# Reciprocal roots by ScalarE's square root and one Newton step, and softmax maxima negated by the reduction and scaled by ScalarE

## The chip, the cores and the metric

The kernel runs on one core of a Trainium2 chip. The metric is the device time of one execution in microseconds; where several executions of a kernel are timed, their median counts. The engines of the core are named as in the profile: PE is TensorE's matmul and PEld its weight load, DVE is VectorE, ACT is ScalarE, POOL is GpSimd and SP is SyncE, which issues most of the transfers.

## What is computed

Two blocks of two layers each over 512 tokens of width 1024. The first block has a second stream of 256 context tokens. What matters here are its root mean square norms, its softmaxes and the places where they stand:

```python
def rmsnorm(x, gain=None):
    xf = x.astype(jnp.float32)
    y = xf * lax.rsqrt(jnp.mean(xf * xf, axis=-1, keepdims=True) + EPS)
    ...

def attend(q, k, v):
    s = jnp.einsum('bkgqd,bksd->bkgqs', q, k).astype(jnp.float32) * (HEAD_DIM ** -0.5)
    p = jax.nn.softmax(s, axis=-1).astype(v.dtype)
    return jnp.einsum('bkgqs,bksd->bkgqd', p, v)

def first_block(...):
    for l in range(DEPTH):
        ...
        hx = rmsnorm(x) * (1 + sc_a) + sh_a
        hc = rmsnorm(ctx) * (1 + mc[1]) + mc[0]
        ...                       # mixer: Fourier, attention (normed heads), gated recurrence
        x = x + g_a * (jnp.concatenate([fx, ax, rx], axis=-1) @ w_out[l])
        x = x + g_f * swiglu(rmsnorm(x) * (1 + sc_f) + sh_f, w_gate[l], w_up[l], w_down[l])
        ...
    return rmsnorm(x, final_norm)

def second_block(...):
    for l in range(DEPTH):
        hdn = swiglu_2(rms_norm(x, norm_pre[l, 0]), ...)
        x = x + 0.5 * rms_norm(hdn, norm_post[l, 0])
        ...                       # l = 0: block attention (MoBA) and a linear recurrence; l = 1: a convolution
        x = x + rms_norm(mix, norm_post[l, 1])
        hdn = swiglu_2(rms_norm(x, norm_pre[l, 2]), ...)
        x = x + 0.5 * rms_norm(hdn, norm_post[l, 2])
    return x
```

## The kernel before

Activations are kept feature by feature: 8 tiles of 128 features, with the tokens along the free axis. Every fp32 product is made of three matmuls on rounded halves (lines 245 to 247): a value is split into a rounded high part, by an ACT copy, and the rest, by a DVE subtraction (`split`, lines 212 and 213; weights at lines 230 and 232, once they have landed).

The program is a row of phases: the first mixer (Mix1, layer 0), its feed-forward block ffn0, the second mixer (layer 1), ffn1, and then four feed-forward blocks (ffn2) with two other mixers between them: MixE with MoBA and a linear recurrence, MixO with a convolution. Inside a mixer several streams (dense projections, two halves of the recurrence `hgrn`, Fourier, attention) are woven together by declared costs. Between two phases `boundary` runs: the last products of a phase for one chunk of 256 tokens are followed by the norm and the splits of the next phase for that chunk, while TensorE goes on with the other chunk.

A norm runs so: ACT squares the tiles (line 297), POOL or DVE adds them (line 299), PE sums over features by a product with a column (line 311), `rsqrt_small` makes the reciprocal root of a few columns, DVE spreads it (line 284), PE transposes it (line 286), and then it multiplies tiles. `rsqrt_small` begins with the addition of EPS (line 269, or 271 with a column). Lines 272 and 273 make a first guess from the bits of the number, and a loop of three Newton steps follows (lines 275 to 277): 12 DVE operations on 2 to 12 columns. It is called 51 times: once in the opening, 16 times in the two mixers (heads of keys and queries, `hgrn`), and otherwise in norms at the phase boundaries.

`softmax_tile` handles 128 queries against all their keys: the maximum of a row (line 562, DVE), the negative scaled maximum (line 565 where the scale is the constant 0.125, line 567 where it is a column), and on ACT the exponential, which takes both and also adds up the row (line 568). There are 80 such tiles with a column (attention of the two mixers) and 32 with the constant (MoBA). The exponentials are transposed by PE (line 1011).

A buffer comes from one of two hand-run stores, `arena` and `rarena`, with a third part, `room`, that is lent to either. The order in which the instructions of an engine stand is set when the program is built, by a scheduler that runs a timeline of its own over the dependencies; so a change at one place can move instructions elsewhere. The build puts an ACT table load ahead of an ACTIVATE whose function is not in the set that was loaded last.

Of the kernel before, what the change touches and what calls it, by code (L numbers as in the profile page):

```python
# [10 lines left out]
I32 = mybir.dt.int32  # L11
U8 = mybir.dt.uint8
AF = mybir.ActivationFunctionType
ALU = mybir.AluOpType
AX = mybir.AxisListType
# [48 lines left out]
class _Arena:  # L64
# [32 lines left out]
    def fr(self, *bufs):  # L97
        for b in bufs:
            if isinstance(b, (list, tuple)):
                self.fr(*b)  # L100
                continue
            h = b.home
            assert (h.freed[b.o:b.o + b.u] == np.inf).all()
            h.clock += 1
            h.freed[b.o:b.o + b.u] = h.clock
# [38 lines left out]
def _body(tc, xc, cvec, w_ada, w_in, w_four, w_out, gu, dn, cols, ab_in, ab_out, gates, c_in, c_out,  # L144
          k_id, k_hs, k_lm, k_cm, k_dft, k_dftc, k_bd, k_rope, xsc, out, stop=None, dbg=None, mark=lambda n: None):
    nc = tc.nc
    V, A, G, PE, SP = nc.vector, nc.scalar, nc.gpsimd, nc.tensor, nc.sync
# [9 lines left out]
    with es:  # L157
# [34 lines left out]
        def hlrows(n, count):  # L192
            r = [(alr(n, True), alr(n, True)) for _ in range(count)]
            return r, r
# [12 lines left out]
        def pick(tag):  # L207

            return G if tag in ONPOOL else V

        def split(h, lo, src, eng=V):
            A.activation(h, src, AF.Copy)  # L212
            eng.tensor_tensor(lo, src, h.bitcast(F32), ALU.subtract)  # L213
# [50 lines left out]
        def rsqrt_small(ps, n, eps=None):  # L264

            b = al(192)
            v, y, t = (b.f[:, i * 64:i * 64 + n] for i in range(3))
            if eps is None:
                V.tensor_scalar(v, ps, EPS, None, op0=ALU.add)
            else:  # L270
                V.tensor_tensor(v, ps, eps, ALU.add)
            V.tensor_scalar(t.bitcast(I32), v.bitcast(I32), 1, None, op0=ALU.logical_shift_right)
            V.tensor_scalar(y.bitcast(I32), t.bitcast(I32), -1.0, float(0x5F3759DF), op0=ALU.mult, op1=ALU.add)
            for _ in range(3):
                V.tensor_tensor(t, v, y, ALU.mult)
                V.scalar_tensor_tensor(t, t, -0.5, y, op0=ALU.mult, op1=ALU.mult)
                V.scalar_tensor_tensor(y, t, 1.5, y, op0=ALU.add, op1=ALU.mult)
            return b, y

        def bcast_r(r, ps, tb, c, heads):  # L280
# [88 lines left out]
        class Ffn(Phase):  # L369
# [11 lines left out]
            def begin(self, ch):  # L381
                if self.act is None:
                    mark(self.name)
                    self.actb, self.act = hlrows(self.w, KD)
                if self.beginf:
                    self.beginf(ch)

# [155 lines left out]
        def rope(xs, tabs, shift, tag):  # L543
            n = S
            sh, m1 = al(n), al(n)
            V.stream_shuffle(sh.f, xs, shift)
            G.tensor_tensor(m1.f, xs, tabs[0].f, ALU.mult)
            pick("r1" + tag).tensor_tensor(sh.f, sh.f, tabs[1].f, ALU.mult)
            pick("r2" + tag).tensor_tensor(xs, m1.f, sh.f, ALU.add)
            fr(sh, m1)  # L550
# [7 lines left out]
        def softmax_tile(sp, nk, sc, pn, sm):  # L558

            b = al(64)  # L560
            mx, nb = (b.f[:, i:i + 1] for i in range(2))
            V.reduce_max(mx, sp[:, :nk], axis=AX.X)
            if sc is None:
                sc = 0.125
                V.tensor_scalar(nb, mx, -sc, None, op0=ALU.mult)
            else:
                V.scalar_tensor_tensor(nb, mx, -1.0, sc, op0=ALU.mult, op1=ALU.mult)
            A.activation(pn, sp[:, :nk], AF.Exp, bias=nb, scale=sc, accum_out=sm)
            fr(b)

# [747 lines left out]
        class MixE(Mix2):  # L1318
# [36 lines left out]
            def dense(self):  # L1355
# [40 lines left out]
                for j in range(4):  # L1396
                    for d, b in ((self.q, j), (self.k, 4 + j)):
                        f = al(S)
                        self.proj(b, f.f)
                        rope(f.f, self.rope, sh8, "E")  # L1400
                        d[j], = hlrows(S, 1)[0]
                        split(d[j][0].r, d[j][1].r, f.f, pick("seE"))
                        fr(f)
                        yield 5.2
                    f = al(S)
                    self.proj(8 + j, f.f)
                    pt = transposed(f.f, S)
                    fr(f)
                    v = self.v[j] = alr(1024, True)
                    vr = v.r.rearrange("p (t g c) -> p t g c", t=4, g=2)  # L1410
                    vf = v.f.rearrange("p (t g c) -> p t g c", t=4, g=2)
                    for t in range(4):
                        src = pt.f[:, t * 128:t * 128 + 128].rearrange("p (g c) -> p g c", g=2)
                        A.activation(vr[:, t, :, 0:64], src, AF.Copy)
                        V.tensor_tensor(vr[:, t, :, 64:128], src, vf[:, t, :, 0:64], ALU.subtract)
                    pf_(pt)
                    self.flags.add(f"qkv{j}")
                    yield 5.2
# [488 lines left out]
```

## Time and profile before

| what | value |
|---|---|
| median of 3 runs | 3865.65 us (3865.28 to 3867.86) |
| the profiled execution: its time, its span | 3867.11 us, 3865.3 us |
| mean granted clock of TensorE | 0.972 |
| instructions | 49381 |
| ACT table loads in the program | 15 |

Everything that is read from a trace comes from the one profiled execution. Times in it count from the start of the span. A row of a timeline gives the start, the duration, the engine, the source line and the operation, what it writes and reads with shapes, how many instructions the row merges, and in brackets how long the engine had been idle before and what ended that. A busy PE is not a PE at its peak, since matmuls overlap.

### The profile page before, as it was taken

How to read it: one execution, taken by the hardware profiler on the slowest of the kernel's cores; microseconds unless marked ns; L12 is line 12 of the kernel's file. 1: busy time of each engine (PE TensorE's matmuls, PEld its weight loads, DVE VectorE, ACT ScalarE, POOL GpSimd, SP SyncE). 2: the span in 40 equal slices, each digit the busy share in tenths (PEclk: the TensorE clock that was granted, in tenths of full speed). 3: DMA queues.
4: the chain of work that ended last, by engine and by line, in shares of the span. 5: the costliest groups of instructions: out<-in, count | busy, mean ns of one | idle time of the engine just before them, and what ended most of it. 6: DMA issues, size and time to landing. Idle time of an engine off the chain costs nothing.

```text
span 3865.3 us, 49381 instructions
## 1 busy us (share of the span) xinstructions
PE 3669.9 (95%) x19960; PEld 3152.5 (82%) x19960; DVE 1955.3 (51%) x3502; ACT 1350.5 (35%) x2265; POOL 571.9 (15%) x507
## 2 busy tenths in 40 slices
PE   6988799999999888999999998999999999999998
PEld 5776688888887767888988896798889888888887
DVE  8687756533245676433442357653336333735233
ACT  4234643432233355322332234443224222323231
POOL 3332112431013310000100031030002001211001
PEclk9898999999999899999999998999999999999999
DMA  5222104443211212332233222123323322323222
GB/s 203 65 89 66 58 30 158 157 139 132 67 43 53 60 54 82 97 98 80 71 112 101 67 86 74 50 88 109 102 73 99 104 95 74 107 70 100 94 94 73
DMA packets 95829, 345.18 MB, mean 89 GB/s; under 512 B 10864, under 2 KB 14064, under 8 KB 95600
## 3 DMA queue, kind: packets, MB, share of 16 engines
q1 hardware_dynamic: 95024, 341.50, 27.4%
q8 instruction: 156, 2.56, 0.3%
q14 instruction: 73, 0.60, 0.0%
q10 hardware_dynamic: 576, 0.52, 0.0%
HBM read 334.64 MB, written 4.19 MB: 88 GB/s over the span
## 4 chain that ended last, share of the span: by engine, by line
PE 57%; DVE 3%; ACT 1%; DMA 1%; POOL 0%; issue 0%; DVEq 0%; POOLq 0%; ACTq 0%; SPq 0%
PE psum L245 17%; PE psum L246 17%; PE psum L247 17%; DVE rarena L1168 1%; PE psum L262 1%; PE psum L261 1%; PE psum L260 1%; PE psum L311 1%; PE psum L1477 1%; DVE arena L1213 1%; DMA arena<-gu 0%; POOL arena L1215 0%; DVE rarena L232 0%; PE psum L1491 0%; PE psum L1011 0%
## 5 line engine op out<-in xcount | busy, mean ns | idle before, releaser
L245 PE MATMUL psum<-rarena,room 128*128 128x512 f32 (+1 forms) x3041 | 1073.2, 354 | 18.0 <-ACT rarena L212 8.5
L246 PE MATMUL psum<-rarena,room 128*128 128x512 f32 (+1 forms) x3041 | 1073.0, 353 | 3.8 <-DVE rarena L213 2.3
L247 PE MATMUL psum<-rarena,room 128*128 128x512 f32 (+1 forms) x2955 | 1052.7, 357 | 0.8 <-DVE room L232 0.8
L247 PE MATMUL psum<-rarena 128*128 128x512 f32 (+1 forms) x2118 | 743.7, 352 | 11.6 <-DVE rarena L232 11.5
L245 PE MATMUL psum<-rarena 128*128 128x512 f32 (+1 forms) x2032 | 727.7, 359 | 17.8 <-ACT rarena L230 7.7
L246 PE MATMUL psum<-rarena 128*128 128x512 f32 (+1 forms) x2032 | 725.2, 357 | 1.3 <-DVE rarena L213 1.3
L245 PEld LDWEIGHTS psum<-rarena,room 128*128 128x128 f32 x3041 | 579.2, 191 | 97.0 <-ACT rarena L212 8.7
L246 PEld LDWEIGHTS psum<-rarena,room 128*128 128x128 f32 x3041 | 579.5, 191 | 80.6 <-DVE rarena L213 2.8
L247 PEld LDWEIGHTS psum<-rarena,room 128*128 128x128 f32 x2955 | 562.5, 190 | 79.9 <-DVE room L232 1.0
L232 DVE TENSOR_TENSOR room<-arena,room 128x1024 fp32r<-128x1024 f32 (+2 forms) x252 | 325.2, 1297 | 519.2 <-PE psum L246 207.6
L230 ACT ACTIVATE room<-arena 128x1024 fp32r<-128x1024 f32 (+2 forms) x290 | 319.5, 1110 | 664.0 <-PE psum L247 169.1
L299 POOL TENSOR_TENSOR arena<-arena 128x256 f32<-128x256 f32 x170 | 144.4, 856 | 2286.3 <-ACT arena L297 2065.0
L247 PEld LDWEIGHTS psum<-rarena 128*128 128x128 f32 x2118 | 407.7, 193 | 63.8 <-DVE rarena L232 12.8
L245 PEld LDWEIGHTS psum<-rarena 128*128 128x128 f32 x2032 | 391.9, 193 | 73.6 <-ACT rarena L230 8.8
L246 PEld LDWEIGHTS psum<-rarena 128*128 128x128 f32 x2032 | 391.7, 193 | 52.6 <-DVE rarena L213 1.5
L230 ACT ACTIVATE rarena<-arena 128x1024 fp32r<-128x1024 f32 (+2 forms) x141 | 157.7, 1123 | 361.6 <-PE psum L247 89.7
L232 DVE TENSOR_TENSOR rarena<-arena,rarena 128x1024 fp32r<-128x1024 f32 (+2 forms) x104 | 137.5, 1322 | 262.6 <-ACT rarena L230 129.3
L212 ACT ACTIVATE rarena<-arena 128x256 fp32r<-128x256 f32 (+2 forms) x254 | 130.3, 530 | 241.4 <-DVE arena L410 202.6
L213 DVE TENSOR_TENSOR rarena<-arena,rarena 128x256 fp32r<-128x256 f32 (+2 forms) x247 | 143.0, 596 | 95.9 <-ACT rarena L212 95.8
L410 DVE TENSOR_TENSOR arena<-arena,psum 128x512 f32<-128x512 f32 (+1 forms) x170 | 100.2, 598 | 176.5 <-PE psum L247 168.2
L297 ACT ACTIVATE arena<-arena 128x256 f32<-128x256 f32 (+1 forms) x274 | 107.0, 412 | 211.2 <-DVE arena L1239 87.6
L500 POOL TENSOR_TENSOR arena<-arena 128x1024 f32<-128x1024 f32 x48 | 120.7, 2521 | 230.8 <-DMA arena<-w_ada 141.1
(360 smaller groups left out, 4234.1 us busy)
## 6 DMA issues: line engine op xcount, KB each, us to landing
arena<-gu SPq DMA_DIRECT2D x264, 512.0 KB, 3.7
arena<-dn SPq DMA_DIRECT2D x80, 704.0 KB, 4.1
arena<-w_ada SPq DMA_DIRECT2D x57, 512.0 KB, 3.8
room<-w_ada SPq DMA_DIRECT2D x39, 512.0 KB, 3.7
room<-w_in SPq DMA_DIRECT2D x31, 512.0 KB, 3.6
arena<-c_in SPq DMA_DIRECT2D x24, 512.0 KB, 3.5
arena<-dn SPq DMA_DIRECT2D x16, 448.0 KB, 3.8
room<-ab_in SPq DMA_DIRECT2D x13, 512.0 KB, 3.6
```

Source lines behind the costliest of these rows:

```text
L212: A.activation(h, src, AF.Copy)
L213: eng.tensor_tensor(lo, src, h.bitcast(F32), ALU.subtract)
L230: A.activation(h.r, r.f, AF.Copy)
L232: (G if wlo[1] < wlo[0] else V).tensor_tensor(lo.r, r.f, h.f, ALU.subtract)
L245: PE.matmul(ps, h[:, s], ah, start=k == 0, stop=False)
L246: PE.matmul(ps, h[:, s], al_, start=False, stop=False)
L247: PE.matmul(ps, lo[:, s], ah, start=False, stop=k == nk - 1)
L260: PE.matmul(o, w[0].r[:, s], ah, start=False, stop=False)
L297: A.activation(sq.f, src, AF.Square)
L299: (V if self.fast else G).tensor_tensor(self.parts[0].f, self.parts[0].f, sq.f, ALU.add)
L410: V.tensor_tensor(s.f, s.f, pu, ALU.mult)
L500: G.tensor_tensor(t.f, r.f, sic[q].f, ALU.mult)
```

## The change

`rsqrt_small` loses the guess from the bits and two of the three Newton steps. In their place ACT takes a square root, DVE a reciprocal, and one Newton step follows: five DVE operations with the addition at its head, and one on ACT. In `softmax_tile` the reduction negates the maximum itself. Where the scale is a column, ACT multiplies by it. Where it was the constant 0.125, nothing is multiplied; instead MoBA's queries are scaled when they are split, which takes the factor along in the ACT copy and makes the DVE subtraction one of three operands. In ffn0, whose head has one hidden tile, the rows for it are allocated at the start of the phase instead of at its first head.

```diff
--- before.py
+++ after.py
@@ -269,12 +269,11 @@
                 V.tensor_scalar(v, ps, EPS, None, op0=ALU.add)
             else:
                 V.tensor_tensor(v, ps, eps, ALU.add)
-            V.tensor_scalar(t.bitcast(I32), v.bitcast(I32), 1, None, op0=ALU.logical_shift_right)
-            V.tensor_scalar(y.bitcast(I32), t.bitcast(I32), -1.0, float(0x5F3759DF), op0=ALU.mult, op1=ALU.add)
-            for _ in range(3):
-                V.tensor_tensor(t, v, y, ALU.mult)
-                V.scalar_tensor_tensor(t, t, -0.5, y, op0=ALU.mult, op1=ALU.mult)
-                V.scalar_tensor_tensor(y, t, 1.5, y, op0=ALU.add, op1=ALU.mult)
+            A.activation(y, v, AF.Sqrt)
+            V.reciprocal(y, y)
+            V.tensor_tensor(t, v, y, ALU.mult)
+            V.scalar_tensor_tensor(t, t, -0.5, y, op0=ALU.mult, op1=ALU.mult)
+            V.scalar_tensor_tensor(y, t, 1.5, y, op0=ALU.add, op1=ALU.mult)
             return b, y
 
         def bcast_r(r, ps, tb, c, heads):
@@ -382,6 +381,8 @@
                 if self.act is None:
                     mark(self.name)
                     self.actb, self.act = hlrows(self.w, KD)
+                    if self.hf == 1:
+                        self.hid = hlrows(self.w, 1)[0]
                 if self.beginf:
                     self.beginf(ch)
 
@@ -558,13 +559,12 @@
         def softmax_tile(sp, nk, sc, pn, sm):
 
             b = al(64)
-            mx, nb = (b.f[:, i:i + 1] for i in range(2))
-            V.reduce_max(mx, sp[:, :nk], axis=AX.X)
+            nb = b.f[:, 0:1]
+            V.reduce_max(nb, sp[:, :nk], axis=AX.X, negate=True)
             if sc is None:
-                sc = 0.125
-                V.tensor_scalar(nb, mx, -sc, None, op0=ALU.mult)
+                sc = 1.0
             else:
-                V.scalar_tensor_tensor(nb, mx, -1.0, sc, op0=ALU.mult, op1=ALU.mult)
+                A.activation(nb, nb, AF.Copy, scale=sc)
             A.activation(pn, sp[:, :nk], AF.Exp, bias=nb, scale=sc, accum_out=sm)
             fr(b)
 
@@ -1399,7 +1399,11 @@
                         self.proj(b, f.f)
                         rope(f.f, self.rope, sh8, "E")
                         d[j], = hlrows(S, 1)[0]
-                        split(d[j][0].r, d[j][1].r, f.f, pick("seE"))
+                        if d is self.q:
+                            A.activation(d[j][0].r, f.f, AF.Copy, scale=0.125)
+                            V.scalar_tensor_tensor(d[j][1].r, f.f, 0.125, d[j][0].f, op0=ALU.mult, op1=ALU.subtract)
+                        else:
+                            split(d[j][0].r, d[j][1].r, f.f, pick("seE"))
                         fr(f)
                         yield 5.2
                     f = al(S)
```

What the scheduler makes of it is shown at three places. First VectorE in the opening, around the first root. `mod` holds the modulation columns, made by products with rows of w_ada. Before:

```order
L269 TENSOR_SCALAR arena<-psum 128x6
L272 TENSOR_SCALAR arena<-arena 128x6
L273 TENSOR_SCALAR arena<-arena 128x6
L275 TENSOR_TENSOR arena<-arena 128x6
L276 SCALAR_TENSOR_TENSOR arena<-arena 128x6
...
L1641 SCALAR_TENSOR_TENSOR room,mod_65<-room,arena 128x1024
...
L1648 TENSOR_SCALAR mod_65<-psum,COL 128x2
...
L284 COPY room<-arena 128x128 x6
```

After:

```order
L269 TENSOR_SCALAR arena<-psum 128x6
L273 RECIPROCAL arena<-arena 128x6
L274 TENSOR_TENSOR arena<-arena 128x6
L275 SCALAR_TENSOR_TENSOR arena<-arena 128x6
L276 SCALAR_TENSOR_TENSOR arena<-arena 128x6
L283 COPY room<-arena 128x128 x6
L1645 SCALAR_TENSOR_TENSOR room,mod_65<-room,arena 128x1024 x2
```

Two products with w_ada and their additions, which stood inside the chain, now stand behind the copies that end it (line 1645 is line 1641 of before).

Second ScalarE in the attention of the first mixer, beside the readout of `hgrn` (lines 943 and 944 copy and square its output). Before:

```order
L568 ACTIVATE room,arena<-psum,room,arena 128x768
L568 ACTIVATE room,arena<-psum,arena 128x768
L943 ACTIVATE room<-psum 128x256
L944 ACTIVATE room<-psum 128x256
L212 ACTIVATE rarena<-psum 128x512 x6
```

After:

```order
L568 ACTIVATE room,arena<-psum,room,arena 128x768
L943 ACTIVATE room<-psum 128x256
L944 ACTIVATE room<-psum 128x256
L567 ACTIVATE arena<-arena 128x1
L272 ACT_TABLE_LOAD
L272 ACTIVATE room<-room 128x4
L568 ACT_TABLE_LOAD
L568 ACTIVATE room,arena<-psum,arena 128x768
L212 ACTIVATE rarena<-psum 128x512 x6
```

A scaled maximum (line 567) stands ahead of its exponential, and between the two are the root of the readout and two table loads.

Third ScalarE at a boundary between two ffn2 blocks (1183 copies a broadcast root out of PSUM, 407 and, after, 408 is the silu). Before:

```order
L230 ACTIVATE room<-arena 128x1024
L1167 ACTIVATE rarena<-arena,COL 128x256
L297 ACTIVATE arena<-arena 128x256 x2
L1183 ACTIVATE arena<-psum 128x256
L407 ACTIVATE arena<-arena 128x256 x3
L212 ACTIVATE rarena<-arena 128x256 x3
L230 ACTIVATE room<-arena 128x1024 x3
```

After:

```order
L1183 ACTIVATE arena<-psum 128x256
L408 ACT_TABLE_LOAD
L408 ACTIVATE arena<-arena 128x256 x3
L212 ACTIVATE rarena<-arena 128x256 x3
L230 ACTIVATE room<-arena 128x1024 x3
L272 ACT_TABLE_LOAD
L272 ACTIVATE arena<-arena 128x2
L230 ACTIVATE rarena<-arena 128x1024
```

The table is changed for the silus and back for the next root; before, no load stood here. In the whole program there are 52 loads where there were 15.

## Rows read from the trace of the kernel before

**Rows 1.** Page, part 1: busy time of each engine, its share, instructions.
```profile
PE 3669.9 (95%) x19960; PEld 3152.5 (82%) x19960; DVE 1955.3 (51%) x3502; ACT 1350.5 (35%) x2265; POOL 571.9 (15%) x507
```
**Rows 2.** Windows: length, busy PE, PEld, DVE, ACT, POOL, clock, DMA.
```profile
0.00:100.00 100.00, 65.44 (x325) 56.49 (x327) 84.30 (x120) 45.70 (x68) 35.10 (x20) 0.97 0.57 197
260.00:500.00 240.00, 196.42 (x1056) 154.99 (x1055) 172.69 (x368) 123.37 (x250) 41.51 (x33) 0.89 0.18 55
1310.00:1530.00 220.00, 194.16 (x1081) 160.74 (x1080) 141.81 (x260) 111.44 (x209) 33.38 (x30) 0.94 0.18 55
2600.00:2850.00 250.00, 250.00 (x1105) 207.07 (x1104) 91.92 (x99) 74.75 (x90) 0.00 (x0) 1.00 0.30 98
```
**Rows 3.** Waits of PE: us in total, times, longest.
```profile
PE psum L1011 <- ACT room L568: 26.8, 24, 3.6
...
PE psum L1000 <- ACT room L568: 13.8, 10, 3.4
...
PE psum L286 <- DVE arena L284: 9.8, 9, 2.7
...
PE psum L286 <- DVE room L284: 6.7, 2, 3.5
```
**Rows 4.** Windows, DVE busy: lines 275, 276, 277, 272, 273, 567 in turn.
```profile
0.00:3865.30 3865.30, 41.79 (x153) 0.97 0.28 89
0.00:3865.30 3865.30, 33.35 (x153) 0.97 0.28 89
0.00:3865.30 3865.30, 35.28 (x153) 0.97 0.28 89
0.00:3865.30 3865.30, 18.98 (x51) 0.97 0.28 89
0.00:3865.30 3865.30, 20.63 (x51) 0.97 0.28 89
0.00:3865.30 3865.30, 17.23 (x80) 0.97 0.28 89
```
**Rows 5.** Timeline of DVE: first and last operation of the last chain.
```profile
3853.42 0.16 DVE L271 TENSOR_TENSOR arena<-psum,arena 128x2 f32<-128x2 f32 x1 [1.59 <-PE psum L311]
...
3855.59 0.16 DVE L277 SCALAR_TENSOR_TENSOR arena<-arena 128x2 f32<-128x2 f32 x1
```
**Rows 6.** Groups by line: operations on few columns (busy us, mean ns).
```profile
L579 DVE RECIPROCAL arena<-arena 128x8 f32<-128x8 f32 (+1 forms) x16 | 3.1, 195 | 12.4 <-ACT room L568 8.5 <-ACT arena L568 3.8
...
L1302 ACT ACTIVATE arena<-COL 128x4 f32<-128x4 f32 x1 | 0.2, 206 | 0.0
```
**Rows 7.** Timeline: from a scaled maximum to its exponential.
```profile
442.75 0.16 DVE L567 SCALAR_TENSOR_TENSOR room<-room,arena 128x1 f32<-128x1 f32 x1
...
443.00 0.99 ACT L568 ACTIVATE room<-psum,room,arena 128x768 f32<-128x768 f32 x1 [2.42 <-DVE room L567]
```
**Rows 8.** Timelines of DVE and POOL: inside the opening's chain.
```profile
18.94 2.19 DVE L273 TENSOR_SCALAR arena<-arena 128x6 int32<-128x6 int32 x1
...
29.35 0.36 DVE L284 COPY room<-arena 128x128 f32<-128x128 f32 x2
...
18.76 2.34 POOL L1643 TENSOR_TENSOR room<-room,arena 128x1024 f32<-128x1024 f32 x1 [18.32 <-DVE arena L269]
```
**Rows 9.** Timeline of ACT: two table loads and what follows.
```profile
1141.84 1.28 ACT L645 ACT_TABLE_LOAD   x1
1143.98 0.38 ACT L645 ACTIVATE arena<-psum 128x256 f32<-128x256 f32 x1 [0.86 <-PE psum L247]
...
2570.31 1.28 ACT L407 ACT_TABLE_LOAD   x1
2571.61 1.03 ACT L407 ACTIVATE arena<-arena 128x256 f32<-128x256 f32 x3
```
**Rows 10.** Timeline of PE: stalls ahead of two phases.
```profile
1151.86 0.80 PE L245 MATMUL psum<-rarena,room 128*128 128x256 f32 x2 [4.19 <-ACT rarena L212]
...
1543.48 1.44 PE L245 MATMUL psum<-rarena,room 128*128 128x256 f32 x5 [4.30 <-ACT rarena L212]
```

## The prediction

> **What bounds the kernel now.** I read the busy shares first: TensorE is busy for 95% of the span, VectorE for 51%, ScalarE for 35% [rows 1]. So the change, which touches no matmul, can only act on the 195 us in which TensorE stands still (3865.3 - 3669.9). The table by stage says where these are [rows 2]: 34.6 us in the first 100, 43.6 in the first mixer's attention (260 to 500), 25.8 in the second mixer's (1310 to 1530), and none in the middle of a feed-forward block (250.00 of 250). Then the waits of TensorE say for whom [rows 3]: for the exponentials of line 568 on ScalarE (26.8 + 13.8 us), and at line 286, the transposes that broadcast a reciprocal root (9.8 + 6.7 us). The change works on both.
>
> **What the roots cost, and what takes their place.** There are 51 calls of rsqrt_small. Lines 272 and 273 run once a call, lines 275 to 277 three times; together they hold VectorE for 41.79 + 33.35 + 35.28 + 18.98 + 20.63 = 150.0 us [rows 4]. An undisturbed chain is the last one: from 3853.42 to 3855.75, 2.33 us for 12 operations, 0.194 each [rows 5]. The new chain has 5 VectorE operations (the addition, the reciprocal, three of the one step), so 0.97 us; the reciprocal is taken at that size since line 579's took 0.195 [rows 6]. A square root on a few columns is priced by line 1302, 0.21 us [rows 6]. A crossing from VectorE to ScalarE takes 0.09 (line 567 ends at 442.91, line 568 starts at 443.00 [rows 7]), and there are two. That makes 1.36 us, 0.97 less than before, if ScalarE is free and has the right table. Disturbed chains lose more: the opening's took 10.4 us from line 273 at 18.94 to the copies of line 284 at 29.35, because single operations stood for some 2 us while GpSimd multiplied (line 273 for 2.19, until 21.13; GpSimd's ran until 21.10 [rows 8]), and fewer operations meet fewer of these. VectorE loses about 150.0 - 51 x 4 x 0.194 = 110 us, and 80 x 0.215 = 17 more at line 567 [rows 4]; the 32 at line 565 are taken at the same size, 7.
>
> **What ScalarE gains.** 51 roots and 80 scaled maxima at 0.21 are 27.5 us. The order shows 52 table loads where there were 15; a load takes 1.283, shown as 1.28 [rows 9], so 37 more are 47.5 us. Altogether 75 us on an engine that is 65% idle. A load stands behind what precedes it on ScalarE, but need not wait for the operand: at 1141.84 one ran 0.86 us ahead of its matmul [rows 9]. Most new loads stand like that in the order, so most are hidden while ScalarE idles. The Trainium skill speaks against this change: "ScalarE: Activation LUTs", section "Table sets: the hidden batching unit", says to group calls by table set, and this change alternates roots with exponentials, sigmoids and silus. The same page, section "What ACT_TABLE_LOAD costs", has 2.66 us a switch, with a drain; by it the 37 loads would be an estimated 98 us. The row at 2571.61 disagrees: the next ACTIVATE began 0.02 us after its load had ended [rows 9].
>
> **The sum, place by place.**
> 1. *Opening.* What is left of the chain after line 273's start shrinks from 10.4 us to about 1.2, or 3.4 with one collision of 2.2. The load is behind the silus of line 1663 and has no wait of its own. What is late next are the products with w_ada on VectorE, which is 84% busy there [rows 2] and loses about 7 us of work too. Bounds 0 and -7 (10.4 - 3.4); I take **-5**, nearer to the gain since VectorE sets the pace there.
> 2. *End.* Behind the last chain TensorE waits 2.7 us, the longest of its waits in [rows 3] at line 286 for the arena, and nothing covers it; both last roots share one load. **-1**.
> 3. *Other waits at line 286.* 9.8 + 6.7 - 3.5 - 2.7 (the two longest, terms 1 and 2) = 10.3 us in nine places; VectorE is full there with the scaled copies around the chain, and 7 of 12 chain operations go. But the root now queues behind ScalarE's squares and splits. Bounds 0 and -10.3; **-5**.
> 4. *Norms ahead of the second mixer and of its feed-forward block.* TensorE waits 4.19 and 4.30 us for splits that a root chain precedes [rows 10]. Five more loads fall near the first of these. Bounds +3 (two loads exposed) and -8.5; **-3**.
> 5. *Softmax in the two mixers.* Before: maximum, 0.16 on VectorE, 0.09, exponential [rows 7]. After: maximum, 0.09, 0.21 on ScalarE, exponential on the same engine. The chain keeps its length within 0.1 us, so its 80 tiles give nothing directly. VectorE, the busier engine here (172.69 against 123.37 us of 240 [rows 2]), gets lighter. Against that the order puts a root with its two loads between exponentials three times (2 x 1.28 + 0.21 = 2.8 us each, 8.3 in all). Bounds: +30 (80 x 0.21 = 16.8, the 8.3, and the mixers' four other new loads, 5.1, all exposed) and -25 (VectorE's relief ends over a third of the 69 us of idle TensorE); I take **-2**, near nought because the rows put TensorE's waits about as much on ScalarE as on VectorE.
> 6. *MoBA.* 32 times one VectorE operation less ahead of the exponential, 0.19 each, 6 us if nothing hid them; TensorE has other streams to run: **-1**. The four query splits only take a factor along, on the same engines: 0.
> 7. *Boundaries between feed-forward blocks.* 26 of the new loads, up to four at one boundary. TensorE has whole products queued there, and a silu load stood at 2570.31 in the kernel before [rows 9] while line 407 is nowhere among the engines that TensorE waited for. **0**; without that cover 26 x 1.28 = +33, of which I leave a few us in the range. The earlier allocation of ffn0's first hidden rows only changes an address: 0.
>
> Together -17 us. The profiled execution took 3867.11 us (span 3865.3 and 1.8 around it), 1.5 above the median of 3865.65; from the median, **3849 us**. Its own spread: 3838 to 3857.9, from half of terms 1, 3 and 4 to all of them.
>
> **The rivals.**
> A. *Hidden.* The roots' waits are filled by the next late thing (a weight split, a w_ada load), only the end and a part of the opening remain: -1 - 5, 3860 us. For it: TensorE's queue is in order, and what stands ahead of line 286 is often late as well. Against it: line 286 is named as a wait of its own eleven times.
> B. *ScalarE becomes the late engine in the mixers (slower).* The copies and loads of term 5 sit in ScalarE's order between exponentials, and TensorE already waits 40.6 us for these [rows 3]. All exposed: +30, less the 14 us of terms 1 to 4: 3882 us. It decides from nearly three quarters exposed: (14 + 7.7) of 30. For it: the waits by name. Against it: ScalarE is 51% busy in these windows.
> C. *VectorE's relief counts fully.* Term 5 at -25: 3826 us. For it: VectorE is at 72% in the first attention and its operations are the ones that GpSimd stalls. Against it: about half the waits end on ScalarE.
> D. *A load also empties ScalarE.* Were each to cost its 1.28 once more, the ten in the mixers would add 12.8 us: -17 + 13, 3862 us. The row at 2571.61 [rows 9] speaks against it. The drain is the skill's rule, "What ACT_TABLE_LOAD costs" again.
> That the change would not do what it says is out: the order has the 51 reciprocals and 80 scaled copies.
>
> **How the numbers follow.** Forecast 0.42, A 0.20, B 0.17, C 0.17, D 0.04. A measurement of this kernel tells about 0.2% (7.7 us) from no change. Faster: forecast and C, 0.59; same: A and D, 0.24; slower: B, 0.17. The range of 3822 to 3876 holds forecast, A and D, two thirds of C and a third of B, and leaves out 0.17.
>
> **What would show it.** Right: TensorE's wait at line 286 down from 16.5 us to under 8; the opening's copies of line 284 some 7 us earlier; VectorE's busy time down by 110 to 140 us, ScalarE's up by 70 to 80; last root chain about 1.4 us. Wrong: TensorE waiting more than 45 us for line 568 (B); silu or sigmoid loads named as releasers at the block boundaries (term 7); those copies no earlier than 27 us (term 1); idle time behind every load (D).

## The result, and the profile after

| | before | after |
|---|---|---|
| median | 3865.73 us | 3817.85 us (3813.81 to 3824.42) |
| ratio to before | | 0.9877, 95% interval 0.9860 to 0.9894 |
| profiled execution: time, span | 3867.11, 3865.3 us | 3813.81, 3811.9 us |
| TensorE busy, and the rest of the span | 3669.9, 195.4 us | 3644.4, 167.5 us |
| mean granted clock | 0.972 | 0.977 |

The change saves 48 us, where 17 were forecast; 3817.85 lies 4 us below the range's lower end of 3822. The lines have moved: 286 is now 285, 284 is 283, 562 is 563, 1701 is 1705, 272 is ScalarE's root, 273 the reciprocal and 567 ScalarE's scaled copy.

Part 1 of the page of the kernel after answers to [rows 1]:

```profile
PE 3644.4 (96%) x19960; PEld 3135.4 (82%) x19960; DVE 1879.7 (49%) x3033; ACT 1426.0 (37%) x2433; POOL 576.0 (15%) x507
```

ScalarE gained 75.5 us (75 were worked out), VectorE lost 75.6 (110 to 140 were). The number of matmuls is the same, yet TensorE is busy for 25.5 us less and stands still for 27.9 less: the 53.4 us of the span come from both by halves. The profiled execution is the fastest of the four. Over all four the granted clock was 0.974 to 0.977 with a mean of 0.976, over all executions of the kernel before 0.969 to 0.975 with a mean of 0.972. The product of busy time and clock, of which more below, was 3567 and 3561 us. An estimate from these for the 48 us between the medians is some 20 for the busy time (3567/0.972 - 3561/0.976) and 28 for the stand-still. That the busy time of untouched matmuls would fall was nowhere in the prediction.

TensorE's waits (engine, line, who was waited for: us in total, times, longest us). Before, beside [rows 3]:

```profile
PE psum L247 <- DVE rarena L232: 11.5, 3, 5.8
...
PE psum L1701 <- ACT rarena L1693: 3.7, 2, 3.0
```

After:

```profile
PE psum L1011 <- ACT room L568: 24.8, 24, 2.7
PE psum L1705 <- ACT rarena L1697: 10.6, 2, 6.8
PE psum L285 <- DVE arena L283: 9.7, 9, 3.0
PE psum L247 <- DVE rarena L232: 6.4, 2, 5.8
...
PE psum L1000 <- ACT room L568: 3.6, 6, 1.5
...
PE psum L285 <- DVE room L283: 1.6, 2, 0.9
```

The wait at the transposes went from 16.5 to 11.3 us, not to under 8. The wait of line 1000, whose products need the place that an exponential frees, went from 13.8 to 3.6. The wait of the opening for the splits of line 1697 (1693 before) grew from 3.7 to 10.6.

Three stages by windows, cut at the same instructions: the dense part of mixer 2, the first attention, and the second, which follows that dense part. Before (window, length, then busy us and count of PE, PEld, DVE, ACT, POOL, the granted clock, DMA share, GB/s):

```profile
1179.80:1335.70 155.90, 145.35 (x774) 121.27 (x775) 83.96 (x178) 44.41 (x85) 55.39 (x63) 0.89 0.17 53
277.10:498.30 221.20, 177.62 (x946) 138.72 (x945) 163.22 (x355) 113.63 (x233) 38.18 (x32) 0.88 0.19 59
1335.70:1488.40 152.70, 126.86 (x699) 101.19 (x699) 113.43 (x224) 86.68 (x166) 21.45 (x17) 0.91 0.19 58
```

After:

```profile
1162.80:1304.70 141.90, 139.19 (x775) 116.38 (x776) 74.43 (x136) 47.63 (x93) 55.13 (x63) 0.95 0.19 58
268.50:480.50 212.00, 168.74 (x953) 132.28 (x952) 155.84 (x293) 131.02 (x287) 36.68 (x32) 0.92 0.19 60
1304.70:1443.90 139.20, 121.91 (x699) 99.41 (x698) 106.53 (x183) 96.92 (x200) 21.45 (x17) 0.94 0.20 62
```

These three give 14.0, 9.2 and 13.5 us, 36.7 of the 53.4 (the first attention begins 8.6 us earlier, and the stages behind the second give the rest), and in each the granted clock rose. In the first attention TensorE stands still as long as before (43.6 and 43.3 us); all that it gained there is matmuls at a higher clock.

**A stand-still with a low clock behind it.** The dense part of mixer 2 has one stall of before that the prediction didn't speak of. TensorE waits 5.85 us for a weight split (line 232). The rows of TensorE, of ScalarE and of VectorE show what stood ahead of it. ScalarE had rounded the weight by 1293.63 (line 230); VectorE first worked on two chains of reciprocal roots, one behind the other, some of their operations 1.2 us long.

```profile
1301.07 0.79 PE L247 MATMUL psum<-rarena 128*128 128x512 f32 x1 [5.85 <-DVE rarena L232]
```

```profile
1292.57 1.06 ACT L230 ACTIVATE rarena<-room 128x1024 fp32r<-128x1024 f32 x1 [1.24 <-issue]
```

```profile
1296.02 0.17 DVE L277 SCALAR_TENSOR_TENSOR arena<-arena 128x8 f32<-128x8 f32 x1
1296.22 0.26 DVE L804 TENSOR_SCALAR arena<-arena 128x8 f32<-128x8 f32 x1
1296.30 0.18 DVE L269 TENSOR_SCALAR arena<-psum 128x8 f32<-128x8 f32 x1
1296.54 0.17 DVE L272 TENSOR_SCALAR arena<-arena 128x8 int32<-128x8 int32 x1
1296.74 1.28 DVE L273 TENSOR_SCALAR arena<-arena 128x8 int32<-128x8 int32 x1
1298.06 1.18 DVE L275 TENSOR_TENSOR arena<-arena 128x8 f32<-128x8 f32 x1
...
1299.79 1.22 DVE L232 TENSOR_TENSOR rarena<-room,rarena 128x1024 fp32r<-128x1024 f32 x1
```

The windows of 5 us around it, before, and then the same place after:

```profile
1290.00:1295.00 5.00, 4.04 (x26) 3.18 (x25) 4.83 (x11) 3.38 (x5) 2.96 (x3) 1.00 0.71 238
1295.00:1300.00 5.00, 0.22 (x2) 0.13 (x2) 4.64 (x13) 1.06 (x1) 3.11 (x6) 0.51 0.19 76
1300.00:1305.00 5.00, 3.93 (x9) 3.14 (x10) 5.00 (x11) 0.00 (x0) 3.10 (x2) 0.50 0.01 2
1305.00:1310.00 5.00, 5.00 (x22) 4.07 (x21) 2.53 (x14) 1.54 (x2) 1.20 (x2) 0.97 0.00 0
```

```profile
1270.00:1275.00 5.00, 4.88 (x22) 3.71 (x21) 4.42 (x10) 2.22 (x4) 0.81 (x5) 1.00 0.26 102
1275.00:1280.00 5.00, 5.00 (x27) 4.25 (x26) 4.53 (x7) 1.75 (x3) 4.16 (x3) 1.00 0.00 0
```

While TensorE stands still the granted clock is at a half (the 1.2 GHz level), and it is still there when the matmuls come back: 9 in 3.93 us, where windows at 1.00 hold 22 to 27 in 5. After, with seven operations fewer in each chain on VectorE, the stall is about 0.1 us and the clock stays at 1.00. The experiments below bear this out: this stall stands in each of the ten profiled kernels that have the long chains (5.68 to 5.85 us, with the clock at 0.50 in it and behind it), and in none of the ten with shorter ones, whatever their order and their softmax. The longest wait for line 232 after is another one, 5.84 us at 2319.60, which had 4.74 us before (at 2371.22).

### The profile page after: what moved, and what is told of

Same layout as the page of the kernel before. It is cut to its first block, busy times and chain, and to the rows that moved or that the text cites. A ratio compares the mean times of both kernels' runs of the same rounds, so it can differ in the third digit from the quotient of the medians.

```text
span 3811.9 us, 49051 instructions
## 1 busy us (share of the span) xinstructions
PE 3644.4 (96%) x19960; PEld 3135.4 (82%) x19960; DVE 1879.7 (49%) x3033; ACT 1426.0 (37%) x2433; POOL 576.0 (15%) x507
## 5 line engine op out<-in xcount | busy, mean ns | idle before, releaser
L247 PEld LDWEIGHTS psum<-rarena 128*128 128x128 f32 x2118 | 404.1, 191 | 58.6 <-DVE rarena L232 8.0
L245 PEld LDWEIGHTS psum<-rarena 128*128 128x128 f32 x2032 | 387.4, 191 | 62.5 <-ACT rarena L230 5.4
L246 PEld LDWEIGHTS psum<-rarena 128*128 128x128 f32 x2032 | 387.8, 191 | 52.0 <-issue 0.7
```

The lines of the kernel that those rows point to most:

```text
L245: PE.matmul(ps, h[:, s], ah, start=k == 0, stop=False)
L246: PE.matmul(ps, h[:, s], al_, start=False, stop=False)
L247: PE.matmul(ps, lo[:, s], ah, start=False, stop=k == nk - 1)
```

## The experiments

Times are medians; the kernel before had 3862 to 3867 in all these comparisons, and gains are against it unless another kernel is named. Waits, busy times and clocks come from one profiled execution each. The granted clock of one and the same kernel differs between executions (0.969 to 0.975 before), so that a busy time is uncertain by some 11 us (3567/0.969 - 3567/0.972).

**The parts alone.** First the new roots, without the softmax:

```diff
-            V.tensor_scalar(t.bitcast(I32), v.bitcast(I32), 1, ...)
-            V.tensor_scalar(y.bitcast(I32), t.bitcast(I32), -1.0, ...)
-            for _ in range(3):       # three Newton steps
+            A.activation(y, v, AF.Sqrt)
+            V.reciprocal(y, y)       # and one Newton step
```

> The kernel before with the new reciprocal roots alone (softmax, query split and allocation as before). Theory V: VectorE has fewer operations in the mixers and the woven streams there run closer together, whoever waits for whom; the roots take about 110 of the 135 us that VectorE loses, so most of the 48 us comes from them: 3832 us (-34). Theory S: the softmax sets the mixers' pace and the roots only give what the prediction said for the opening, the end and the waits at line 286: 3853 us (-12). Theory O: the gain is the scheduler's order by luck; anything between 3820 and 3880 with no relation to the work removed.

Measured: 3848.42, ratio 0.9954 (0.9938 to 0.9969), 18 us. Then shorter roots without ScalarE (coarser, two of the three Newton steps are left out):

```diff
-            for _ in range(3):
+            for _ in range(1):
```

> The kernel before with one Newton step instead of three after the guess from the bits: 6 VectorE operations of 12 go, ScalarE gets nothing, no table load. It leaves two steps of the root out, so the roots are coarse. Theory V: at least what the new roots give, since as many VectorE operations go and no root waits for ScalarE: 3828 us. Theory S: 3852 us. If the loads and ScalarE's queue cost something, this one is faster than the new roots by that: 0 to 15 us.

Measured: 3841.60, ratio 0.9933 (0.9912 to 0.9954), 25 us. Both lie between what the two theories gave, the change's own roots nearer to the smaller gain; they are worth more than terms 1 to 4 say (14 us). The softmax of the two mixers alone:

```diff
-                V.reduce_max(mx, sp[:, :nk], axis=AX.X)
-                V.scalar_tensor_tensor(nb, mx, -1.0, sc, op0=ALU.mult, op1=ALU.mult)
+                V.reduce_max(nb, sp[:, :nk], axis=AX.X, negate=True)
+                A.activation(nb, nb, AF.Copy, scale=sc)
```

> The kernel before with the new softmax of the two mixers alone (80 tiles: negated maximum, ScalarE scales it; MoBA and the roots as before). Theory V: VectorE loses 17 us of 1955, ScalarE gains 16.5: 3860 us (-5). Theory S: the exponential no longer stands behind another maximum on VectorE, TensorE's 40.6 us of waits for line 568 fall by half and the clock with it: 3840 us (-25).

Measured: 3844.19, ratio 0.9940 (0.9923 to 0.9957), 23 us. Term 5 said 2. MoBA's part alone (negated maximum, scaled queries):

```diff
-                sc = 0.125
-                V.tensor_scalar(nb, mx, -sc, None, op0=ALU.mult)
+                sc = 1.0
...
+                        if d is self.q:
+                            A.activation(d[j][0].r, f.f, AF.Copy, scale=0.125)
```

> The kernel before with MoBA's part alone (32 tiles without the multiplication, queries scaled when split). Theory V: 3862 us (-4, the stage from MixE's start to the end of MoBA got 6 us shorter in the full change). Theory S: 3859 us. The prediction's own term 6: -1.

Measured: 3866.76, ratio 0.9997 (0.9985 to 1.0009): nothing, as term 6 had it. ffn0's earlier allocation wasn't run alone; that it costs nothing is not shown.

**Why the softmax gains.** Three variants of the softmax part in the two mixers, against the line `A.activation(nb, nb, AF.Copy, scale=sc)` above. The multiplication back on VectorE:

```diff
+                V.tensor_tensor(nb, nb, sc, ALU.mult)
```

> The softmax tiles of the two mixers only: the reduction negates the maximum, but the multiplication by the column stays on VectorE, as many operations as before. Three theories for the 23 us that the softmax part alone gave. Q (queue): the scaled maximum used to stand in VectorE's queue behind other operations, 0.87 and 0.83 us a tile, and on ScalarE it follows at once; then this kernel gains nothing: 3866, within 6. R (relief): VectorE has 80 operations, 17 us, less; then nothing here either: 3866, within 6. O (order): any edit lets the scheduler set another order, and that alone moves the time by some 20 us; then it lies anywhere from 3840 to 3885.

Measured: 3861.38, ratio 0.9994 (0.9983 to 1.0005): no gain. The negation alone is worth nothing; where the multiplication stands is what counts. On GpSimd:

```diff
+                G.tensor_tensor(nb, nb, sc, ALU.mult)
```

> The softmax tiles of the two mixers only: negated maximum, and the multiplication by the column on GpSimd instead of VectorE. R (relief): VectorE is as light as with ScalarE's copy, so the gain is kept: 3844, within 6. Q (queue): the scaled maximum now stands in GpSimd's queue, behind multiplications of 1 to 2 us, and needs two crossings, so the time from the maximum to the exponential is no shorter than before, and the gain is gone: 3866 or more, up to 3890. O (order): anywhere from 3840 to 3885.

Measured: 3844.14, ratio 0.9948 (0.9932 to 0.9963). The gain is kept, so my expectation of the queue theory failed: GpSimd's queue is mostly empty in the attentions (busy for 38.18 of 221.20 us in the first, before). And a second copy behind the scaled one:

```diff
+                A.activation(mx, nb, AF.Copy, scale=sc)
+                A.activation(nb, mx, AF.Copy)
```

> The softmax tiles of the two mixers only, as in the change, with a second small copy on ScalarE behind the scaled one, so that each exponential comes one ScalarE operation (0.21 us, 80 in all, 16.8 us) later. Q (queue): the gain was 23 us for about 0.6 us a tile that the exponential came earlier, so a third of it goes: 3852, from 3848 to 3858. R (relief): VectorE is as light as in the change and ScalarE has room: 3844, within 4. The prediction's rival B (ScalarE is late): all 16.8 us show, 3861.

Measured: 3861.70, ratio 0.9985 (0.9976 to 0.9994): 18 of the 23 us are gone again. From the rows of the reduction and the exponential in both attentions (the n-th of one with the n-th of the other, 48 + 32 tiles) I added up the time from the end of a maximum to the start of its exponential:

| kernel | 80 tiles, us | TensorE's wait of line 1000 for an exponential | TensorE not busy | time against before |
|---|---|---|---|---|
| before | 121.7 | 13.8 | 195.4 | |
| e5_neg | 118.8 | 13.6 | 192.0 | -0.06% |
| e7_twice | 98.0 | 6.2 | 184.4 | -0.15% |
| e3_softmix | 60.9 | 3.4 | 182.7 | -0.60% |
| e6_pool | 52.2 | 2.6 | 179.9 | -0.52% |
| e1_roots | 119.4 | 14.3 | 172.6 | -0.46% |

In the first five lines the first three columns of numbers go together: the sooner the exponential, the less TensorE waits. That VectorE is lighter does not do it by itself: e1_roots takes 66 us off VectorE and leaves both numbers of the softmax as they were (it stands still less for the sake of the roots). One tile of before shows where the time was. VectorE's rows, and ScalarE's exponential:

```profile
336.43 0.41 DVE L562 TENSOR_REDUCE room<-psum 128x1 f32<-128x256 f32 x1
336.88 0.69 DVE L574 TENSOR_TENSOR arena<-psum,room 64x512 f32<-64x512 f32 x1
338.22 0.59 DVE L873 COPY_PREDICATED room<-lm,psum 128x384 f32<-128x384 uint8 x1 [0.66 <-PE psum L868]
338.70 1.21 DVE L498 SCALAR_TENSOR_TENSOR room<-room,arena 128x1024 f32<-128x1024 f32 x1
339.84 0.09 DVE L498 DVE_READ_ACCUMULATOR room<-room,arena 128x1 f32 x1
339.84 0.58 DVE L873 COPY_PREDICATED room<-lm,psum 128x384 f32<-128x384 uint8 x1
340.31 0.15 DVE L567 SCALAR_TENSOR_TENSOR room<-room,arena 128x1 f32<-128x1 f32 x1
```

```profile
340.49 0.56 ACT L568 ACTIVATE room<-psum,room,arena 128x256 f32<-128x256 f32 x1 [4.09 <-DVE room L567]
```

The maximum is ready at 336.84. The scheduler set other streams' work ahead of the 0.15 us that still lack, and the exponential starts 3.65 us later, while ScalarE has been idle for 4.09. A tile of the same size after, on VectorE and then on ScalarE:

```profile
327.06 0.42 DVE L563 TENSOR_REDUCE room<-psum 128x1 f32<-128x256 f32 x1
327.40 0.75 DVE L213 TENSOR_TENSOR rarena<-psum,rarena 128x256 fp32r<-128x256 f32 x2
```

```profile
327.52 0.29 ACT L567 ACTIVATE room<-room,arena 128x1 f32<-128x1 f32 x1 [0.69 <-DVE room L563]
327.84 0.56 ACT L568 ACTIVATE room<-psum,room,arena 128x256 f32<-128x256 f32 x1
```

Now 0.36 us. The Trainium skill, "Perfetto Trace Analysis", section "Optimizing Scalar/DVE Operations", says that where VectorE is saturated, moving some work to ScalarE or even GpSimd may make sense, and that a move to GpSimd might not help, since it shares a read port with VectorE. Here VectorE was not saturated (163.22 of 221.20 us), and the gain did not come from its relief; and for operations of one column the move to GpSimd helped as much (e6_pool).

The last column doesn't follow the others so well: e7_twice stands still hardly longer than e3_softmix (184.4 and 182.7 us), and takes 17 us more. The windows of the two attentions, e3_softmix and then e7_twice, show where:

```profile
276.20:481.50 205.30, 167.33 (x953) 131.75 (x952) 158.48 (x307) 125.83 (x281) 37.51 (x32) 0.93 0.20 62
1317.10:1461.80 144.70, 126.06 (x698) 102.77 (x698) 108.77 (x191) 94.77 (x198) 21.44 (x17) 0.91 0.20 62
```

```profile
276.50:496.80 220.30, 182.14 (x946) 144.44 (x945) 157.33 (x307) 133.91 (x329) 36.73 (x32) 0.84 0.19 59
1334.40:1479.90 145.50, 124.05 (x699) 99.84 (x697) 108.11 (x190) 99.41 (x229) 21.45 (x17) 0.94 0.19 59
```

In the first attention both stand still for 38 us (205.30 - 167.33 and 220.30 - 182.14), but one is granted 0.93 and the other 0.84, and the same matmuls take 15 us longer. In these two executions waits of the same sum, lying elsewhere, went with another clock; why these lie worse is not shown.

**Order alone.** So I changed nothing but the place of a buffer:

```diff
-            b = al(192)
+            b = al(256)
```

> The kernel before with one neutral edit: the small buffer of a reciprocal root has 256 columns instead of 192, of which the same columns are used. No instruction is added or taken away; buffers lie elsewhere and the scheduler sets another order in many places. Q and R: 3866, within 6. O (order): anywhere from 3845 to 3885; the distance from 3866 says how much of a difference between two of these kernels needs no other cause than the order.

Measured: 3904.71, ratio 1.0106 (1.0087 to 1.0126), 38 us slower with the same instructions; the scheduler had set 1621 of TensorE's in another order. And smaller:

```diff
-            b = al(192)
-            v, y, t = (b.f[:, i * 64:i * 64 + n] for i in range(3))
+            b = al(64)
+            v, y, t = (b.f[:, i * 16:i * 16 + n] for i in range(3))
```

> The kernel before with the small buffer of a reciprocal root at 64 columns instead of 192 (the three vectors stand 16 columns apart instead of 64). No instruction is added or taken away. With 256 columns it was 38 us slower. P (place): a larger buffer waits longer for a free place in the stores, so a smaller one is the faster: 3866 or less, down to 3830. O (order): the scheduler's order alone did it, which this edit upsets as well (3971 instructions of TensorE stand in another order, 1621 with 256 columns), so the time can go either way by some 40: 3826 to 3906, with no sign to expect.

Measured: 3883.16, ratio 1.0054 (1.0038 to 1.0071), 21 us slower. Larger and smaller both lose, so it isn't room in the stores (P) but the order. The whole change with the small buffer:

> The whole change, with the small buffer of a root at 64 columns instead of 192; no instruction is added or taken away against the change. If its 48 us are the shorter chains alone: 3818, within 6. O (order): the change's own order was a lucky draw, and another order of the same work lies anywhere from 3800 to 3858. P (place): a smaller buffer gains a few us: 3800 to 3818.

Measured: 3807.95, ratio 0.9853 (0.9837 to 0.9870), 10 us less than the change. This put the question whether the 48 us are the change's or its order's, and the parts were run in all three orders:

> The whole change with the root's buffer at 256 columns. Against 3905 for the same buffer without the change: if the gain belongs to the shorter chains, it is 48 to 75 us as in the other two buffer sizes: 3830 to 3857. If the change only took away a bad order's waits or had a lucky order of its own: anywhere between 3800 and 3905.

> The new roots alone, buffer of 64 columns; against 3883 without them. Own mechanism: 18 us as with 192 columns, 3865, within 6. The order has a share: any other gain, from -20 to +60.

> The softmax of the two mixers alone, buffer of 64 columns; against 3883 without it. Own mechanism: 23 us as with 192 columns, 3860, within 6. The order has a share: any other gain, from -20 to +60.

> The new roots alone, buffer of 256 columns; against 3905 without them. Own mechanism alone: 18 to 28 us as in the other two orders, 3877 to 3887. If the roots are what takes away the bad orders' waits: 50 us or more, 3855 or less.

> The softmax of the two mixers alone, buffer of 256 columns; against 3905 without it. Own mechanism alone: 18 to 23 us as in the other two orders, 3882 to 3887. If the softmax is what takes away the bad orders' waits: 50 us or more, 3855 or less.

Medians in us, and in brackets TensorE's time not busy and its busy time in the profiled execution:

| root's buffer | neither part | softmax of the mixers | roots | whole change |
|---|---|---|---|---|
| 192 columns | 3866 (195, 3670) | 3844 (183, 3661) | 3848 (173, 3678) | 3818 (168, 3644) |
| 64 columns | 3883 (199, 3692) | 3865 (190, 3673) | 3855 (177, 3675) | 3808 (173, 3637) |
| 256 columns | 3905 (209, 3688) | 3874 (195, 3683) | 3849 (180, 3661) | 3811 (165, 3643) |

Read along a row: the softmax gains 23, 18 and 30 us, the roots 18, 28 and 56, the whole 48, 75 and 94. Every gain has the same sign in every order, so the change is no lucky draw; without it the first order was the lucky one. The stand-still falls by much the same in all three: 9 to 14 us for the softmax, 22 to 29 for the roots. What swings is the busy time: the roots alone lengthen it by 8 us in one order and shorten it by 27 in another, a swing of 35 us where one execution is uncertain by some 11. That is the clock: the product of busy time and mean granted clock lies between 3557 and 3570 us in each of the profiled kernels. Where the roots are new, the three orders lie within 7 to 10 us of each other, where they are old within 30 to 39: with the long chains on VectorE the time depends on the order more than with the short ones.

**The price of the loads.** The whole change, with a short root on VectorE instead of ScalarE's:

```diff
-            A.activation(y, v, AF.Sqrt)
-            V.reciprocal(y, y)
+            V.tensor_scalar(t.bitcast(I32), v.bitcast(I32), 1, ...)
+            V.tensor_scalar(y.bitcast(I32), t.bitcast(I32), -1.0, ...)
```

> The whole change, but the reciprocal root is made of the guess from the bits and one Newton step on VectorE (coarser than before: two of three steps are left out), with no square root on ScalarE, so the 37 further table loads are gone. If the parts add up: 25 us of the coarse root alone plus 23 us of the softmax, 3818, within 6, the same as the change; the loads then cost nothing there either. If the loads and the trips to ScalarE cost 7 us, as the two ways to make roots differ when each is alone: 3811. If order decides: 3780 to 3860.

Measured: 3819.45, ratio 0.9884 (0.9870 to 0.9899). Part 1 of its page:

```profile
PE 3652.9 (96%) x19960; PEld 3143.1 (82%) x19960; DVE 1883.6 (49%) x3084; ACT 1371.1 (36%) x2345; POOL 576.8 (15%) x507
```

ScalarE is 55 us lighter than after, VectorE alike, the time the same: the 37 loads and the 51 roots on ScalarE cost nothing that stands out of the 7 to 10 us between orders. A few us are not excluded: without the new softmax the roots of e1_roots gave 7 us less than those of e2_newton1. And at single places the loads do cost. In the first attention after, the root of line 272 stands with two loads between a scaled maximum and its exponential, as the order showed; ScalarE's rows, and TensorE's:

```profile
349.72 0.29 ACT L567 ACTIVATE arena<-arena 128x1 f32<-128x1 f32 x1 [1.66 <-DVE arena L563]
350.04 1.28 ACT L272 ACT_TABLE_LOAD   x1
351.33 0.20 ACT L272 ACTIVATE room<-room 128x4 f32<-128x4 f32 x1
...
352.85 0.99 ACT L568 ACTIVATE room<-psum,arena 128x768 f32<-128x768 f32 x1
```

```profile
353.98 1.26 PE L1011 MATMUL psum<-ident,room 128*128 128x128 f32 x7 [2.70 <-ACT room L568]
```

The exponential comes 2.84 us behind its scaled maximum, and TensorE waits 2.70 us for it. Five of the 80 tiles have loads there, 10 of the 13 us by which maxima and exponentials lie further apart after than in e3_softmix (74.2 and 60.9 us).

**A faster version.** Without the last Newton step, first in the change's own buffer, then with 64 columns:

```diff
             V.reciprocal(y, y)
-            V.tensor_tensor(t, v, y, ALU.mult)
-            V.scalar_tensor_tensor(t, t, -0.5, y, op0=ALU.mult, op1=ALU.mult)
-            V.scalar_tensor_tensor(y, t, 1.5, y, op0=ALU.add, op1=ALU.mult)
```

> The whole change without its Newton step: square root on ScalarE, then the reciprocal on VectorE, and that is the root (three VectorE operations fewer, 0.58 us a call, 51 calls; as exact as the engine's square root is). If the length of a root's chain counts where TensorE waits for it, about 25 calls at 0.58: 3805 to 3812. If the remaining chains are covered: 3818, within 4. If order decides: 3790 to 3860.

> The whole change without its Newton step and with the buffer of 64 columns, both of which gave 10 us when each was added to the change alone. If both gains are their own: 3798, within 4. If they are the order's, or the same waits: 3808, or anywhere up to 3830.

Measured: 3808.04, ratio 0.9859 (0.9844 to 0.9873), and 3793.99, ratio 0.9810 (0.9795 to 0.9824). Dropping the step gives 10 us in one order and 14 in the other, and the second of these kernels beats both before and after, by 72 and 24 us. Its roots are only as exact as the two engines' square root and reciprocal.

## Why the prediction was right or wrong

**The first bound failed.** "The change, which touches no matmul, can only act on the 195 us in which TensorE stands still." Half of the gain in the profiled executions is outside these: 25.5 us of matmuls at a higher granted clock. Rows 2 had the clock at 0.89 and 0.94 in the mixers, and I read the column only as a description. The sum of -17 was a sum of stand-still; of that there were -27.9.

**Term 5, the softmax in the mixers: -2 taken, -23 measured, of which 13 are stand-still and 9 clock in the profiled executions.** The step that failed is "the chain keeps its length within 0.1 us". It priced the way from the maximum to the exponential by one undisturbed row [rows 7], 0.16 and 0.09 us. The 80 tiles had 1.52 on average, since the scaled maximum stood in VectorE's queue behind other work; with ScalarE's copy it is 0.76 alone, and 0.93 in the whole change. Rival C had nearly the size, with VectorE's relief as its cause; e1_roots shows that a lighter VectorE leaves these waits alone. Nor did rival B come as a whole: line 568 kept TensorE waiting for 28.4 us at lines 1011 and 1000, not for 45; the 2.70 us at 353.98 are of its kind.

**Terms 3 and 4: the sum was fair, the places were not.** The waits at line 286 fell by 5 us in all, opening and end included, where their terms had more. Two of those left, 2.38 us at 2513.23 and 2.96 us at 3256.84, are at block boundaries that had none so long before. At 3256.84 no load is the cause: the root is done on ScalarE at 3251.64, but its reciprocal follows on VectorE only at 3254.24, between scaled copies (line 1168), and the transposes came 58.4 us earlier than before while the products beside them came 52.2 earlier. Of term 4's two stalls the second shrank from 4.30 to 2.81 us, and that stage gave about 2.8 us. The first, at 1151.86, went, but two others stand near its place (2.99 us at 1129.68, 2.20 us at 1146.27), and the dense part behind them begins only 17.0 us earlier where the end of ffn0 was 20.3 us earlier: no gain. But the largest one was neither named nor priced: 5.85 us for line 232 at 1301.07. I looked for those who need a root, and not for those who stand behind its chain on VectorE. With the clock that stage alone gave 14 us. All in all the roots alone gave 18, for 14 in terms 1 to 4.

**Term 1, the opening: right in size.** The copies begin at 21.19, 8.2 us earlier, and the load lies in idle time, as VectorE's and ScalarE's rows show:

```profile
18.16 0.16 DVE L269 TENSOR_SCALAR arena<-psum 128x6 f32<-128x6 f32 x1
...
18.60 0.19 DVE L273 RECIPROCAL arena<-arena 128x6 f32<-128x6 f32 x1 [0.27 <-ACT arena L272]
18.82 1.93 DVE L274 TENSOR_TENSOR arena<-arena 128x6 f32<-128x6 f32 x1
...
21.19 0.91 DVE L283 COPY room<-arena 128x128 f32<-128x128 f32 x6
```

```profile
16.72 1.28 ACT L272 ACT_TABLE_LOAD   x1
18.36 0.21 ACT L272 ACTIVATE arena<-arena 128x6 f32<-128x6 f32 x1 [0.35 <-DVE arena L269]
```

One collision of 1.93 us is left, as assumed. The first products of line 1705 come 11 us earlier; the longer wait for line 1697 takes most of it back, and the recurrence behind them starts 5.4 us earlier, for 5 predicted. Not every product does: some at 111 us come 1.5 us later.

**Term 2, the end: right.** The chain runs from 3801.43 to 3802.67, 1.24 us for 1.36 worked out, and the wait of 2.7 us became 1.6:

```profile
3801.43 0.16 DVE L271 TENSOR_TENSOR arena<-psum,arena 128x2 f32<-128x2 f32 x1 [1.59 <-PE psum L310]
...
3802.51 0.16 DVE L276 SCALAR_TENSOR_TENSOR arena<-arena 128x2 f32<-128x2 f32 x1
```

**Terms 6 and 7: right in the main.** MoBA's part gave 0 (e4_moba). The loads between feed-forward blocks cost nothing that shows: behind 1400 us none runs during a longer wait of TensorE. In sum the 37 further loads of 1.28 us cost nothing that stands out of the 7 to 10 us between orders (e10_n1soft), on a ScalarE that is busy for 37%. The Trainium skill's rule to batch calls by table set ("ScalarE: Activation LUTs", section "Table sets: the hidden batching unit") was worth no more here. Rival D did not come: the root at 351.33 begins 0.01 us behind its load.

**VectorE's busy time** fell by 75.6 us, not 110 or more. The root's lines fell from 150.0 to 50.7 us, by 99 and not by 110, since some of the shorter chain's operations still take far more than 0.194 us (1.93 at 18.82). Part of the rest is that busy time is a union: rows of one engine overlap, as those at 339.84 do. Adding the rows of all lines gives 89.7 us less, where the root's and the scaled maximum's lines gave 122, so other lines also became some 30 us longer; what held them up was not pursued.

**The range.** The prediction's own spread, 3838 to 3857.9, doesn't come out of its terms: with half of terms 1, 3 and 4 the sum gives 3855, with their lower bounds 3836. It would not have held 3818 either way.

**What stays open.** Why a certain order lies badly for the clock was not traced beyond the stall above and the first attention of e7_twice; nor why the clock of the first attention rose (0.88 to 0.92) with as much stand-still as before; nor why the whole gains 7 to 29 us more than its two parts together.

## What to carry to other kernels

Price a link of a chain by the mean distance of its ends over all its instances, not by one clean row: a tiny operation on a busy engine costs its place in that engine's queue, and can go to the engine that waits for it, or to one whose queue is free there. Look for what stands behind an instruction on its engine as well as for who needs its result. Where the granted clock is under 1 in a stage, a stand-still removed may give more than its length; and repeat a part in a second and third order before you put some tens of us down to it.

## What the runs showed of the hardware

In and just behind a stall of 5.85 us the granted clock was 0.50, and 9 matmuls took 3.93 us there. A copy on ScalarE that multiplies one column by another took 0.29 us (line 567 after), where I had priced it at 0.21. One column times another on GpSimd, in an otherwise free queue, led from the maximum to the exponential in 0.56 us (first attention, mean of 48), less than the 0.80 by way of ScalarE (e3_softmix); in the second attention it was 0.80 against 0.70.
